# Last head's output split in place, first w_pm and w_out tiles leaving their last inputs to the end, sums of squares behind other products

## The chip, the cores and the metric

The kernel runs on one core of one Trainium2 chip. The metric is the time of one execution in microseconds on the device; a figure for a kernel is the median of several executions. The engines are named as the profile names them: PE (TensorE, matrix products; PEld is its weight load), DVE (VectorE), ACT (ScalarE), POOL (GpSimd) and SP (SyncE, which here only issues transfers). Each engine works through its own queue of instructions in order, and semaphores make it wait for others.

## The reference, cut to what matters

One layer of a diffusion backbone over 512 latent tokens of width 1024, with 256 context tokens, all in float32:

```python
h = rmsnorm(x, norm1_g) * (1 + sc1) + sh1
hm = head_norm(h_f + h_b, m_norm_g) * o          # mLSTM, 4 heads of width 256, forward and backward
hh = hyena(hv, (hx1, hx2), spec, hy_skip)        # long convolutions
y = gm * (hm @ w_pm) + gh * (hh @ w_ph)          # gated merge
x = x + g1 * (y @ w_out)
h2 = rmsnorm(x, norm2_g) * (1 + sc2) + sh2
x = x + g2 * ((silu(h2 @ w1) * (h2 @ w3)) @ w2)  # FFN, width 2816
return rmsnorm(x, final_g)
```

`g1`, `sh2`, `sc2` and `g2` are columns of `silu(c) @ w_ada + b_ada`. The change is about the way from the last head's `hm` through `w_pm` and `w_out` to `h2` and the first products of the FFN.

## The kernel before, in words

**Layout and products.** Features lie on the 128 partitions, tokens along the free axis; a tile is 128 features by 512 tokens, so a matrix of width 1024 is eight tiles (`KT` = 8). Each float32 operand is split into a high and a low part of a shorter type (`split`, lines 210 to 212: ACT copies the high part, DVE subtracts it for the low one), and each product is made of three PE instructions (`mm3`, lines 214 to 217, hence the lines 215 to 217 in the profile). An output tile is eight inputs times three products of 512 columns, accumulated in one PSUM bank (`gemm`, line 555); its list `ks` says which inputs, and the last product of each `gemm` is noted in `tails`. A block under `behind()` (line 560) puts the instructions that it issues behind the last noted product on PE's queue. Weights come by `wsplit` (line 221): SP loads a raw tile `wr` (four buffers), ACT and DVE split it into `wh` and `wl` (four buffers each).

**Order.** The program is traced as straight code, and a planner then orders the queue of each engine, by the order of tracing as priority and by estimated durations of instructions and transfers; it may pull later work forward into time that it believes free, but keeps the order that `behind()` asks for. Weight loads run at a higher priority. On the chip the queues run in the planned order, whether or not the estimate holds.

**The heads.** For each of four heads, `load_head` loads keys, queries and values (SP, line 894, through the same four `wr` buffers), `decay` builds decay tables, `weigh` multiplies them with the scores (DVE, line 924), `halves` splits the result, `values` makes the outputs of the two directions, and `head_norm` normalises them over a head's width on DVE and POOL (lines 955 to 959). `head_out` (line 961) then transposes the four token tiles on PE (line 965), scales them on ACT (line 968), multiplies them with the output gate that SP has loaded (DVE, line 971) and stores the two feature tiles of the head to DRAM as `hmd` (POOL, line 972). For head h it is called in the course of head h + 1; for the last head by `late()` behind the sixth of the eight `w_ph` tiles. These tiles (`ph_tiles`, line 1272) are spread over the heads as fill for PE. Tiles 0 to 5 of `hmd` are read back and split during the last head (line 1337).

**w_pm.** After the heads, tiles 6 and 7 of `hmd` (the last head's) are read back and split (`reload`, line 1368). Then come eight tiles of `w_pm`, each a whole `gemm`, and a merge: two loads, DVE lines 1379 and 1380, a split into `y`.

**w_out.** Five tiles of `w_out` as whole products, then the last three tiles (`LAST` = 3) in halves of 256 tokens: for each half three products, then the sum of squares over all features by products with ones (`half_rms`, lines 1403 and 1404), a power on POOL (line 373), its spread over the partitions by PE (line 375), and the eight tiles of `h2` for this half (DVE 1438, ACT 1439, DVE 1440). `out_tile` (lines 1390 to 1394) adds the residual and squares. Then the first three FFN tiles, `w1` 0, `w3` 0 and `w1` 1, are made by halves too (lines 1446 to 1450).

**Rows of the modulation matrix.** `background()` takes one step of `ada_later` (line 339): SP loads a 512 KB piece of `w_ada` into a `wr` buffer (line 344), and DVE multiplies the piece loaded before with a row and sums it (line 354). `ada_row` prepares that row. Such steps are called once ahead of the heads, after each `w_ph` tile, after each `w_pm` and `w_out` tile, and three times behind `w_out`; 24 pieces are needed by the end of `w_out`.

## Time and profile before

| | us |
|---|---|
| three runs | 1242.1, 1242.74, 1244.75 |
| median | 1242.74 |
| the profiled execution | 1246.66 |
| its span, first to last instruction | 1244.9 |
| PE busy | 1198.9 (96%) |
| DVE busy | 835.5 (67%) |
| ACT busy | 529.4 (43%) |
| mean granted clock of PE | 0.983 |

The span of the profiled execution starts at 0. The heads run from some 580 us to 755, `w_pm` to 815, `w_out` to 870, the FFN to the end. An engine's busy time says how much work it has; the idle time before an instruction, with what ended it, says what it waited for. The granted clock is 1.00 at full speed (2.4 GHz) and 0.50 at the lower level (1.2 GHz).

### The profile page before, as it was taken

The page shows a single profiled execution, that of the slowest core. Times are in us where ns is not written, and L with a number is a line of the kernel's source. Part 1 is how long each engine was busy: PE and PEld are TensorE (multiplying, and loading weights), DVE is VectorE, ACT ScalarE, POOL GpSimd, SP SyncE. Part 2 cuts the span into 40 slices and gives each one's busy share as a digit, 9 for nine tenths or more (in the row PEclk, how much of TensorE's full clock was granted, in tenths as well). Part 3 has the DMA queues.
Part 4 walks back from the last instruction along what each step waited for, and adds up shares of the span by engine and source line. Part 5 has one row for each costly group of instructions (what it writes and reads, how often), then busy time and mean ns, then how long its engine had stood idle before and what let it go on. Part 6 is the DMA issues. An engine that isn't in the chain of part 4 may idle for free.

```text
span 1244.9 us, 16797 instructions
## 1 busy us (share of the span) xinstructions
PE 1198.9 (96%) x6440; PEld 1020.4 (82%) x6440; DVE 835.5 (67%) x1336; ACT 529.4 (43%) x824; POOL 69.2 (6%) x135
## 2 busy tenths in 40 slices
PE   4999999999999999999999997999999999999997
PEld 2799988888888888887878885878988888888886
DVE  6967798979989899894597785765744433432332
ACT  3754556654445454446564532223422332222231
POOL 0011110100000000001010111000000000000000
PEclk9999999999999999999989997999999999999999
DMA  9644442554342443345435668764443233223312
GB/s 354 236 165 149 160 167 95 181 191 135 112 155 81 161 135 130 116 127 198 139 108 172 209 213 269 260 204 133 147 152 101 87 101 102 91 88 95 104 47 68
DMA packets 61585, 184.83 MB, mean 148 GB/s; under 512 B 8504, under 2 KB 12352, under 8 KB 59328
## 3 DMA queue, kind: packets, MB, share of 16 engines
q1 hardware_dynamic: 53840, 154.38, 38.1%
q0 software_dynamic: 7664, 29.37, 6.4%
q8 instruction: 51, 0.84, 0.3%
q14 instruction: 30, 0.25, 0.1%
HBM read 152.26 MB, written 31.46 MB: 148 GB/s over the span
## 4 chain that ended last, share of the span: by engine, by line
PE 86%; DMA 5%; DVE 4%; issue 2%; ACT 1%; POOL 1%; SPq 0%; DVEq 0%; POOLq 0%; ACTq 0%
PE bank L215 25%; PE bank L216 25%; PE bank L217 25%; DMA wr<-in_wada 3%; PE bank L641 2%; PE bank L642 2%; PE bank L643 2%; DMA s<-hmd 1%; PE bank L862 1%; DVE wl L212 1%; PE bank L445 1%; PE bank L598 1%; PE bank L446 1%; DMA wr<-in_wph 0%; DMA ul<-in_xT 0%
## 5 line engine op out<-in xcount | busy, mean ns | idle before, releaser
L215 PE MATMUL bank<-hTh,wh 128*128 128x512 f32 (+1 forms) x952 | 368.2, 389 | 3.8 <-ACT hTh L1065 2.0
L216 PE MATMUL bank<-hTl,wh 128*128 128x512 f32 (+1 forms) x952 | 367.9, 387 | 1.9 <-DVE hTl L1071 1.9
L217 PE MATMUL bank<-hTh,wl 128*128 128x512 f32 (+1 forms) x952 | 367.2, 386 | 0.0
L211 ACT ACTIVATE wh<-wr 128x1024 fp32r<-128x1024 f32 (+1 forms) x167 | 172.3, 1033 | 431.7 <-PE bank L216 223.1
L212 DVE TENSOR_TENSOR wl<-wr,wh 128x1024 fp32r<-128x1024 f32 (+1 forms) x167 | 198.1, 1188 | 183.0 <-ACT wh L211 181.2
L215 PEld LDWEIGHTS bank<-hTh,wh 128*128 128x128 f32 x952 | 179.7, 189 | 38.9 <-ACT hTh L1065 2.2
L216 PEld LDWEIGHTS bank<-hTl,wh 128*128 128x128 f32 x952 | 179.9, 189 | 36.6 <-DVE hTl L1071 2.4
L217 PEld LDWEIGHTS bank<-hTh,wl 128*128 128x128 f32 x952 | 179.8, 189 | 35.3 <-issue 0.2
L215 PE MATMUL bank<-big,wh 128*128 128x512 f32 (+1 forms) x266 | 96.1, 362 | 7.7 <-ACT big L211 7.7
L216 PE MATMUL bank<-big,wh 128*128 128x512 f32 (+1 forms) x266 | 96.6, 363 | 0.3 <-DVE big L212 0.3
L217 PE MATMUL bank<-big,wl 128*128 128x512 f32 (+1 forms) x266 | 96.0, 361 | 0.0
L215 PEld LDWEIGHTS bank<-big,wh 128*128 128x128 f32 x266 | 51.2, 193 | 15.8 <-ACT big L211 8.6
L216 PEld LDWEIGHTS bank<-big,wh 128*128 128x128 f32 x266 | 51.5, 194 | 8.0 <-DVE big L212 0.7
L217 PEld LDWEIGHTS bank<-big,wl 128*128 128x128 f32 x266 | 51.5, 194 | 7.3
L354 DVE SCALAR_TENSOR_TENSOR wr<-wr,crow 128x1024 f32<-128x1024 f32 x32 | 39.0, 1220 | 22.9 <-DMA wr<-in_wada 22.9
L211 ACT ACTIVATE hb<-hb 128x512 fp32r<-128x512 f32 (+1 forms) x49 | 36.7, 768 | 28.6 <-DVE hb L450 18.2
L1466 DVE TENSOR_TENSOR s<-s,bank 128x512 f32<-128x512 f32 x22 | 15.1, 686 | 46.8 <-PE bank L217 46.8
L212 DVE TENSOR_TENSOR hb<-hb,hb 128x512 fp32r<-128x512 f32 (+1 forms) x49 | 40.3, 858 | 2.0 <-ACT hb L211 1.8
L641 PE MATMUL bank<-wh,hTh 128*128 128x256 f32 (+1 forms) x128 | 36.4, 284 | 0.0
L643 PE MATMUL bank<-wh,hTl 128*128 128x256 f32 (+1 forms) x128 | 36.4, 284 | 0.0
L642 PE MATMUL bank<-wl,hTh 128*128 128x256 f32 (+1 forms) x128 | 36.4, 284 | 0.0
L373 POOL TENSOR_TENSOR rr<-rv,negh 128x2 f32<-128x2 f32 (+1 forms) x6 | 4.5, 756 | 526.4 <-DVE rv L371 526.4
(376 smaller groups left out, 2200.7 us busy)
## 6 DMA issues: line engine op xcount, KB each, us to landing
wr<-in_win SPq DMA_DIRECT2D x64, 512.0 KB, 3.7
wr<-in_w SPq DMA_DIRECT2D x60, 512.0 KB, 3.7
wr<-in_wada SPq DMA_DIRECT2D x32, 512.0 KB, 4.4
Kd<-K POOLq DMA_DIRECT2D x8, 1024.0 KB, 4.7
K<-Kd SPq DMA_DIRECT2D x8, 1024.0 KB, 5.8
wr<-in_wv SPq DMA_DIRECT2D x8, 512.0 KB
gmd<-s POOLq DMA_DIRECT2D x16, 256.0 KB, 2.7
wr<-in_wph SPq DMA_DIRECT2D x8, 512.0 KB, 3.7
```

The costliest lines, as they stand in the source:

```text
L211: act.activation(hi, x, AF.Copy)
L212: dve.tensor_sub(lo, x, hi.bitcast(F32))
L215: pe.matmul(o, wh, xh, start=first, stop=False)
L216: pe.matmul(o, wh, xl, start=False, stop=False)
L217: return pe.matmul(o, wl, xh, start=False, stop=last)
L354: dve.scalar_tensor_tensor(w, w, 1.0, crow[:], op0=ALU.mult, op1=ALU.mult, accum_out=s)
L445: pe.matmul(ps[:], lhs, w4h, start=True, stop=False)
L446: pe.matmul(ps[:], lhs, w4l, start=False, stop=True)
L641: pe.matmul(o, xh, wh, start=bool(k == 0), stop=False)
L642: pe.matmul(o, xh, wl, start=False, stop=False)
L643: m = pe.matmul(o, xl, wh, start=False, stop=bool(k == KT - 1))
L1466: dve.tensor_tensor(t[:], t[:], pb[:], op=ALU.mult)
```

## The change

- `head_out` gets `keep`: with it the two tiles are not stored but handed back.
- The last head's `head_out` is called behind the seventh `w_ph` tile instead of the sixth, with `keep`; its two tiles are split where they are, as inputs 6 and 7 of `w_pm`, before the eighth `w_ph` tile is traced. The reload of these two goes.
- `staged_gemms`: the first n output tiles run their first inputs only, all n; then each runs the remaining inputs, in order, and is finished. For `w_pm` n is 3, with inputs 6 and 7 left to the end; for `w_out` n is 2, with input 7 left.
- In the halves of the last three `w_out` tiles, the first tile of the second half is made before the first half's sum of squares, which is put behind it; the second half's sum is traced after the first FFN half product and put behind it.
- The calls of `background()`: `ada_row` is moved ahead of the first `weigh`; two steps each follow the first `weigh` and the next two fills, and one step follows each `beside`. Those after the `w_ph` tiles, after the first two `w_pm` tiles and behind `w_out` go. Their number stays 25 in all.

```diff
@@ -958,7 +958,8 @@
             gp.tensor_tensor(rs[:], rs[:], negh[:, :1], op=ALU.pow)
             dve.tensor_scalar(hs[:, t], hs[:, t], mv[:, 0:1], rs[:], op0=ALU.subtract, op1=ALU.mult)
 
-    def head_out(h, hs):
+    def head_out(h, hs, keep=False):
+        kept = []
         pt = [bank(), bank()]
         for t in range(4):
             for i in range(2):
@@ -969,7 +970,11 @@
             o = T(PM_, [128, SEQ], F32, "s2")
             dma(o[:], od[:, 2 * h + i])
             dve.scalar_tensor_tensor(hg[:], o[:], 1.0, hg[:], op0=ALU.add, op1=ALU.mult)
-            store(hmd[:, 2 * h + i], hg[:])
+            if keep:
+                kept.append(hg)
+            else:
+                store(hmd[:, 2 * h + i], hg[:])
+        return kept
 
 
     P1 = ExitStack()
@@ -1279,7 +1284,6 @@
             dma(g[:], gmd[:, 1, d])
             dve.scalar_tensor_tensor(g[:], g[:], 1.0, ps[:], op0=ALU.add, op1=ALU.mult)
             store(y2d[:, d], g[:])
-            background()
             yield
 
     fill(next(cf))
@@ -1298,23 +1302,31 @@
         L = heads.get(h) or load_head(h)
         return L, [decay(h, d) for d in range(2)]
 
+    def steps(n):
+        for _ in range(n):
+            background()
+
     L, Dm = start(0)
     fill(next(cf))
+    ada_row()
     weigh(0, L[0], L[1], Dm)
+    steps(2)
     fill(next(cf))
-    ada_row()
+    steps(2)
     W = [halves(Dm[d]) for d in range(2)]
     fill(next(cf))
+    steps(2)
     while fills:
         fill(1)
+        steps(2)
     ph = ph_tiles()
-    background()
     PHN = ((1, 0), (1, 1), (1, 1), (0, 0))
     done = []
 
     def beside(h, i):
         for _ in range(PHN[h][i]):
             next(ph)
+        steps(1)
 
     def late(_=None):
         if done:
@@ -1347,9 +1359,9 @@
         if nxt:
             L, W = nxt[0], Wn
     next(ph)
-    late()
-    for _ in ph:
-        pass
+    next(ph)
+    with behind():
+        ends = head_out(*done.pop(), True)
     PMS.close()
 
 
@@ -1365,13 +1377,36 @@
     def half(t, hf):
         return t[:, 256 * hf : 256 * hf + 256]
 
-    rest = reload(hmd, big, big, range(6, KT))
-    hm = hm[0] + rest[0], hm[1] + rest[1]
+    for t in ends:
+        hi, lo = big(), big()
+        split(hi[:], lo[:], t[:])
+        hm[0].append(hi)
+        hm[1].append(lo)
+    for _ in ph:
+        pass
+
+    def staged_gemms(key, xs, n, last, finish, total, each=1):
+
+        opened = []
+        for d in range(total):
+            wh, wl = wsplit(I[key][d], [128, KT, 128])
+            ps = bank(psG)
+            if d < n:
+                gemm(ps, wh, wl, *xs, SEQ, range(last))
+                opened.append((ps, wh, wl))
+                if d < n - 1:
+                    continue
+                for j, (ps, wh, wl) in enumerate(opened):
+                    with behind():
+                        gemm(ps, wh, wl, *xs, SEQ, range(last, KT))
+                    finish(j, ps)
+            else:
+                gemm(ps, wh, wl, *xs, SEQ)
+                finish(d, ps)
+
     y = ([], [])
-    for d in range(KT):
-        wh, wl = wsplit(I["wpm"][d], [128, KT, 128])
-        ps = bank(psG)
-        gemm(ps, wh, wl, hm[0], hm[1], SEQ)
+
+    def merge(d, ps):
         g = scr()
         dma(g[:], gmd[:, 0, d])
         t = scr()
@@ -1381,7 +1416,10 @@
         y[0].append(big())
         y[1].append(big())
         split(y[0][-1][:], y[1][-1][:], g[:])
-        background()
+        if d > 1:
+            background()
+
+    staged_gemms("wpm", hm, 3, 6, merge, KT)
     dve.tensor_scalar_mul(g1h[:], modT[:, 2, :, 0], 0.5)
 
 
@@ -1414,30 +1452,38 @@
     for d in range(KT):
         xr.append(scr())
         dma(xr[-1][:], I["xT"][:, d])
-        if d < KT - LAST:
-            wh, wl = wsplit(I["wout"][d], [128, KT, 128])
-            ps = bank(psG)
-            gemm(ps, wh, wl, y[0], y[1], SEQ)
-            out_tile(ps, SEQ, d, g1h, 0, xr[d], x1[d], acc1)
-            background()
-    for _ in range(LAST):
+
+    def project(d, ps):
+        out_tile(ps, SEQ, d, g1h, 0, xr[d], x1[d], acc1)
         background()
+
+    staged_gemms("wout", y, 2, KT - 1, project, KT - LAST)
     dve.scalar_tensor_tensor(am2[:], modT[:, 4, :, 0], 1.0, n2g, op0=ALU.add, op1=ALU.mult)
     ws = [wsplit(I["wout"][d], [128, KT, 128]) for d in range(KT - LAST, KT)]
     h2 = ([slots("hTh")() for _ in range(KT)], [slots("hTl")() for _ in range(KT)])
-    for hf in range(2):
-        for d in range(KT - LAST, KT):
-            wh, wl = ws[d - KT + LAST]
-            ps = bank(psG)
-            gemm(ps, wh, wl, [half(t, hf) for t in y[0]], [half(t, hf) for t in y[1]], 256)
-            sq = out_tile(ps, 256, d, g1h, 256 * hf, xr[d], x1[d], acc1)
-        rb = half_rms(acc1, sq, hf)
+
+    def last_tile(hf, d):
+        wh, wl = ws[d - KT + LAST]
+        ps = bank(psG)
+        gemm(ps, wh, wl, [half(t, hf) for t in y[0]], [half(t, hf) for t in y[1]], 256)
+        return out_tile(ps, 256, d, g1h, 256 * hf, xr[d], x1[d], acc1)
+
+    def norm2(hf, sq):
+        with behind():
+            rb = half_rms(acc1, sq, hf)
         for k in range(KT):
             t = scr()
             sh = modT[:, 3, k, 0:1]
             dve.scalar_tensor_tensor(t[:, :256], half(x1[k], hf), am2[:, k : k + 1], rb[:, :256], op0=ALU.mult, op1=ALU.mult)
             act.activation(half(h2[0][k], hf), t[:, :256], AF.Identity, bias=sh)
             dve.scalar_tensor_tensor(half(h2[1][k], hf), t[:, :256], sh, half(h2[0][k], hf).bitcast(F32), op0=ALU.add, op1=ALU.subtract)
+
+    for d in range(KT - LAST, KT):
+        sq = last_tile(0, d)
+    sq1 = last_tile(1, KT - LAST)
+    norm2(0, sq)
+    for d in range(KT - LAST + 1, KT):
+        sq1 = last_tile(1, d)
     ff = ([], [])
     later = ada_later(3 * KT, 4 * KT)
     lead = {}
@@ -1446,6 +1492,8 @@
     for hf in range(2):
         for (n, f), (wh, wl) in zip(jobs, wlead):
             if hf == 0:
+                if len(lead) == 1:
+                    norm2(1, sq1)
                 lead[n, f] = bank(psG)
             gemm(half(lead[n, f], hf), wh, wl, [half(t, hf) for t in h2[0]], [half(t, hf) for t in h2[1]], 256)
```

## Rows read from the trace of the kernel before

**Rows 1.** The page's parts 1 and 2: busy time of each engine and its share of the span; PE's granted clock in 40 slices of the span, in tenths.

```profile
PE 1198.9 (96%) x6440; PEld 1020.4 (82%) x6440; DVE 835.5 (67%) x1336; ACT 529.4 (43%) x824; POOL 69.2 (6%) x135
...
PEclk9999999999999999999989997999999999999999
```

**Rows 2.** The waits of PE over the whole span: line that waited, engine and tile waited for, us in total, times, longest.

```profile
PE bank L215 <- ACT big L211: 7.7, 2, 5.5
...
PE bank L965 <- DVE hs L959: 4.4, 3, 3.0
PE bank L1403 <- DVE s L1394: 2.2, 1, 2.2
```

**Rows 3.** Busy time in chosen stretches: start:end, length, then busy us and count of PE, PEld, DVE, ACT and POOL; granted clock, DMA share, GB/s.

```profile
744.58:767.41 22.83, 18.91 (x76) 14.86 (x74) 15.44 (x30) 6.75 (x9) 6.07 (x8) 0.85 0.77 253
767.41:773.07 5.66, 0.17 (x2) 0.01 (x1) 0.60 (x3) 0.63 (x1) 0.00 (x0) 0.94 0.80 258
773.07:779.20 6.13, 6.13 (x15) 4.79 (x16) 3.25 (x5) 1.69 (x2) 0.00 (x0) 0.50 0.88 313
819.99:823.89 3.90, 1.37 (x5) 0.68 (x5) 3.57 (x6) 0.63 (x1) 0.00 (x0) 0.96 0.82 251
823.89:826.90 3.01, 3.01 (x7) 2.44 (x8) 1.94 (x4) 1.69 (x2) 0.00 (x0) 0.50 0.97 351
```

**Rows 4.** PE in order of time around the last head's transposes (L965) and where w_pm meets the reloaded tiles. Columns: start, duration, engine, line, operation, out<-in, shape, count; in brackets the idle time before it and what ended it.

```profile
744.58 0.38 PE L965 MATMUL bank<-mats,hs 128*128 128x128 f32 x2
...
750.25 0.69 PE L965 MATMUL bank<-mats,hs 128*128 128x128 f32 x2 [3.04 <-DVE hs L959]
...
756.75 0.38 PE L965 MATMUL bank<-mats,hs 128*128 128x128 f32 x2
...
757.66 0.39 PE L215 MATMUL bank<-hTh,wh 128*128 128x512 f32 x1
...
773.07 0.80 PE L215 MATMUL bank<-big,wh 128*128 128x512 f32 x1 [5.49 <-ACT big L211]
```

**Rows 5.** DVE in the same stretch: a row of the modulation matrix (L354), head_norm's last step (L959), head_out's products (L971).

```profile
753.23 1.23 DVE L354 SCALAR_TENSOR_TENSOR wr<-wr,crow 128x1024 f32<-128x1024 f32 x1 [0.53 <-DMA wr<-in_wada]
...
754.91 0.41 DVE L959 TENSOR_SCALAR hs<-hs,mv,rs 128x256 f32<-128x256 f32 x1 [0.45 <-POOL rs L958]
...
761.01 1.29 DVE L971 SCALAR_TENSOR_TENSOR s<-s,s 128x512 f32<-128x512 f32 x2
```

**Rows 6.** POOL and then SP: the store of the last head's two tiles, and the load of the same two.

```profile
762.00 1.15 POOL L972 DMA_DIRECT2D hmd<-s  x2 [7.12 <-DVE s L971]
...
767.38 0.96 SPq L1260 DMA_DIRECT2D s<-hmd  x2
```

**Rows 7.** PE where eight transposes of an earlier head stood together, and a product behind them.

```profile
658.80 1.04 PE L965 MATMUL bank<-mats,hs 128*128 128x128 f32 x8
...
659.92 0.40 PE L216 MATMUL bank<-hTl,wh 128*128 128x512 f32 x1
```

**Rows 8.** PE and then DVE where w_pm ends and w_out begins.

```profile
815.01 0.39 PE L217 MATMUL bank<-big,wl 128*128 128x512 f32 x1
...
819.77 0.39 PE L217 MATMUL bank<-big,wl 128*128 128x512 f32 x1
822.38 0.73 PE L215 MATMUL bank<-big,wh 128*128 128x512 f32 x2 [2.22 <-ACT big L211]
...
818.70 1.22 DVE L354 SCALAR_TENSOR_TENSOR wr<-wr,crow 128x1024 f32<-128x1024 f32 x1
...
823.15 0.69 DVE L212 TENSOR_TENSOR big<-s,big 128x512 fp32r<-128x512 f32 x1
```

**Rows 9.** PE and then DVE around the two halves' sums of squares and the first FFN products.

```profile
856.58 0.28 PE L217 MATMUL bank<-big,wl 128*128 128x256 f32 x1
...
870.26 0.28 PE L215 MATMUL bank<-hTh,wh 128*128 128x256 f32 x1
...
876.00 0.50 PE L1403 MATMUL bank<-mats,s 128*128 128x1 f32 x4
...
889.12 0.40 PE L215 MATMUL bank<-hTh,wh 128*128 128x512 f32 x1
...
855.65 1.23 DVE L354 SCALAR_TENSOR_TENSOR wr<-wr,crow 128x1024 f32<-128x1024 f32 x1 [3.73 <-DMA wr<-in_wada]
...
862.40 0.87 DVE L1438 SCALAR_TENSOR_TENSOR s<-K,am,bank 128x256 f32<-128x256 f32 x2 [2.12 <-PE bank L375]
...
874.49 0.47 DVE L1440 SCALAR_TENSOR_TENSOR hTl<-s,modT,hTh 128x256 fp32r<-128x256 f32 x1
...
878.85 1.26 DVE L1438 SCALAR_TENSOR_TENSOR s<-K,am,bank 128x256 f32<-128x256 f32 x3 [1.58 <-PE bank L375]
```

**Rows 10.** DVE in the first head's stage, the same stretch's busy time (columns as in rows 3), and the idle time of DVE before line 354 over the whole span (us, times).

```profile
594.47 2.58 DVE L924 SCALAR_TENSOR_TENSOR dx<-bank,dx 128x512 f32<-128x512 f32 x4 [12.01 <-PE bank L217]
...
588.00:592.00 4.00, 4.00 (x18) 2.91 (x18) 0.00 (x0) 4.00 (x13) 0.00 (x0) 1.00 0.00 0
...
  DMA wr<-in_wada: 22.9, 14
```

**Rows 11.** Busy time in a stretch of the heads' stage (columns as in rows 3), and PE at a wait in the same stage.

```profile
644.65:656.20 11.55, 10.98 (x38) 8.54 (x39) 8.59 (x24) 7.93 (x21) 3.06 (x4) 0.56 0.45 149
...
719.01 0.47 PE L215 MATMUL bank<-hTh,wh 128*128 128x512 f32 x1 [1.77 <-DVE den L944]
```

## The prediction, made before the changed kernel was run

> **What bounds the kernel now.** I read four views. First the page: PE is busy for 96% of the span, so nothing but PE's own idle or slow time can be won [rows 1]. The clock line shows where to look: two dips, one in the middle (the heads) and none in the long FFN part; full speed is 2.4 GHz, half of it 1.2. Second, the waits of PE: the long ones after the start are the reloaded tiles (big, 7.7 us with 5.5 in one piece), the last head's transposes (hs, 4.4), and the sum of squares (s, 2.2) [rows 2]. Third, busy time by stretch, to see what each wait costs besides itself: behind the 5.66 us gap at 767.41 the granted clock is 0.50 for 6.13 us, so half of that, 3.07, is lost too; behind the gap at 819.99 it is 0.50 for 3.01 us, 1.5 lost [rows 3]. Fourth, the engines in order of time at these places. The full rate is (819.77 - 815.01) / 21 = 0.227 us per product of 512 columns [rows 8]; a tile of 24 takes 5.44.
>
> **The change, part by part.**
>
> *The last head in place (A).* Now the two tiles of head 3 are multiplied on DVE at 761.01, stored by POOL at 762.00, loaded by SP at 767.38, and the first PE product that uses them starts at 773.07 after 5.49 us of idle [rows 4 to 6]. The change drops two stores and two loads (four issues, 256 KB each), keeps the same two splits, and lets the first three w_pm tiles run inputs 0 to 5 first: 3 x 18 x 0.227 = 12.3 us of products that need nothing of head 3, behind the eighth w_ph tile (5.44). The in-place chain is L971 until 762.3, then two splits, of which DVE's half takes 0.69 each (823.15, rows 8) behind ACT's: some 2.1 us in all, ready near 764.4. The inputs would be wanted near 757.66 + 5.44 + 12.3 = 775.4 on the present clock. Cover 11 us, so both the gap and the slow stretch go: 5.66 + 3.07 = **8.7**. If DVE put a row and its DMA wait (1.23 + 3.73, rows 9) ahead, 6 us of cover would be left. Nothing is late next: the finishing parts are 3 x 6 products, and the weights of tile 4 need the buffer pair that tile 0 frees 1.4 us into them, with 2 x 1.4 + 5.44 = 8.2 us to go.
>
> *The transposes one tile later (D).* They stand behind the sixth w_ph tile now; tile 7 is broken up by them. From 744.58 to 757.66 tile 7 and eight transposes take 13.08 us; at full rate they would take 5.44 + 0.9 [rows 4, 7], so 6.7 are lost, to waits for hs and a clock of 0.85 over the stretch [rows 3]. Behind tile 7 they come due at 744.58 + 5.44 = 750.0. But hs of the last token tile is written at 754.91 + 0.41 = 755.3, held by a row on DVE that itself waited for its DMA (753.23) [rows 5]. Everything behind the transposes on PE waits for that: 5.3 us in one piece, and as behind 767.41 a slow stretch of 3.07. Then tile 8 has lost 8.4 instead of 6.7 (a loss of 1.7). If hs came by 750.0 the gain would be the whole 6.7. A gap as short as 1.77 us [rows 11] was followed by full speed; with hs 2 us sooner the gain would be 3.4. Nearest to the rows is hs unchanged, but five matrix rows leave this stage for the first head's, so I take **0** between -1.7 and 6.7.
> By the Trainium skill (TensorE: Matmul & The Clock Gate, section "Part 4: PE-mode transpose") transposes do not count as work for the clock gate, so eight of them in one block would leave the clock down and cost another 3.07, 1232.7 in all. The trace does not bear this out: behind eight together at 658.80 the next product takes 0.40 us, the full-rate duration [rows 7, 8]. So the sum has none of it.
>
> *The first two w_out tiles (B).* The last w_pm product starts at 815.01; its merged tile is split at 823.15 + 0.6 = 823.8, late because rows of the matrix (818.70 among them) stand between its steps on DVE [rows 8]. PE idles 3.90 - 1.37 = 2.5 us and then loses 1.5 [rows 3]. Two tiles without their last input give 2 x 21 x 0.227 = 9.5 us, until 824.8: one us more than needed. **4.0**, at least 0 if a row with its DMA wait (5 us) stands in the way, not more than 4.0.
>
> *Sums of squares (C).* Between 856.7 and 870.26 PE did three half tiles and the small products in 13.5 us; the FFN's six lead products, twice that work, took 889.12 - 870.26 = 18.86, so 9.4 would have done: 4.0 lost [rows 9]. The change puts the sums behind a half tile of 2.9 us. But DVE sets what follows. The sums would start at 859.6 instead of 859.0, so the first half's normalising at 863.0 instead of 862.40, and it takes 874.49 + 0.47 - 862.40 = 12.6 us, because weight splits and the last tiles share DVE: 875.6. The second half's sums must now follow the whole first lead product, whose last inputs are that 875.6: 0.4 us of products, then 2.85 as from 876.00 to 878.85: the second half's normalising starts at 878.8, as now. PE then still has 72 products, 8.6 us, and 0.5 until the first input: 888.0, against 889.12. So of 4.0 only 1.1 is gained; the other 2.9 become a new gap in the lead products. As behind 819.99, that may slow PE and take 1.5 back: -0.4. I take **0.4**, with ends 4.0 and -1.5 (a further row on DVE, 1.22).
>
> *Rows of the matrix moved forward (E).* Five rows and a load more go to the first head's stage: DVE waits 12.01 us before 594.47 and the DMA share is 0.00 at 588 [rows 10]; 5 x 1.23 = 6.1 us fit. Their loads stand on SP ahead of the second head's, and share four buffers with them. Later stages have fewer rows. The nearest wait that they could relieve is 1.77 [rows 11]. I take **0**, between 1.8 gained and the rivals below. The three background steps dropped behind w_out, and those of the w_ph tiles, are the same rows at other places.
>
> **Sum.** 8.7 + 0 + 4.0 + 0.4 + 0 = 13.1. The profiled execution took 1246.66 (span 1244.9), 3.9 above the median; it would be 1233.6. From the median, 1242.74 - 13.1 = **1229.6**.
>
> **The rivals.**
> *hs comes in time.* For it: five rows leave DVE's queue. Against: the waits for the reload of the third head stay. 1229.6 - 6.7 = 1222.9.
> *A new stall in the heads.* There PE has almost no idle, but DVE is full, and in one stretch from 644.65 an idle time of 0.57 was followed by slow products, a clock of 0.56 over 11.55 us, 5.1 lost [rows 11]. The planner orders all queues anew, and one more such stall and D at its lower end give 1229.6 + 5.7 + 1.7 = 1237.0; two give 1242.7, no change.
> *Slower: rows ahead of the first head's weighting.* If the five rows land on DVE behind 594.47 and ahead of the halves that PE waits for, each costs 1.23 and its wait for the load, 22.9 / 14 = 1.6 [rows 10]: 14.3, and a slow stretch of 3.07: 1229.6 + 17.4 = 1247.0. From 13.1 on it decides. Against: the 12 us hole and the idle DMA come first.
> The Trainium skill (PSUM — Partial Sum Buffer, section "Engine vs sequencer instructions") says that the queues of ScalarE and VectorE are strict FIFO, so that such a row holds all behind it. The trace agrees: a row that waited 3.73 us at 855.65 held the tiles behind it and so the sums [rows 2, 9]. With a queue that could be overtaken this rival would fall away.
> *It does not do what it says.* That the split in place hides nothing would need head 3 more than 11 us later than now; I leave it no chance of its own.
>
> **How the numbers follow.** A measurement of this kernel tells 0.2% (2.5 us) from no change. Forecast 0.55, own range 1224 to 1234 (C at 4.0 and some of D below; B gone above). hs in time 0.15. One stall 0.16, two 0.07 (the case of no change). Slower 0.07. Faster: 0.55 + 0.15 + 0.16 = 0.86; same 0.07; slower 0.07. The range 1220 to 1241 leaves out the slower case, the two stalls and a little of hs in time.
>
> **What would show it.** A: no wait of PE for big near the w_pm start, no L972 store for the last head. B: no wait of PE at w_out's first tile. D: eight L965 behind tile 7 with a wait for L959 of 2 to 5 us. C: no wait at L1403 of the first half, but one of hTh or hTl in the lead products. E: five L354 before 600. The prediction is wrong if the heads' stage (580 to 740) lengthens by more than 3 us, or if a wait for big remains.

## The result, and the profile after

The changed kernel took 1237.11 us (median of four, 1236.85 to 1238.27), the kernel before beside it 1243.74 (four, 1242.1 to 1245.43): a ratio of 0.9948 [0.9931, 0.9966], 6.6 us faster. Forecast were 1229.6 and a gain of 13.1, with a range of 1220 to 1241: the time lies within the range, the gain is half of the forecast. In a second comparison (e9 below) the same kernel took 1232.19 against 1246.4, 0.9900 [0.9873, 0.9927]. The title names three parts of the change; a further one, the moved rows of the modulation matrix, turned out to matter as much.

The page of the kernel after, parts 1 and 2 (compare [rows 1]), and the waits of PE that changed or are new (columns as in [rows 2]):

```profile
PE 1196.6 (97%) x6440; PEld 1019.4 (82%) x6440; DVE 835.0 (68%) x1336; ACT 529.4 (43%) x824; POOL 68.2 (6%) x133
...
PEclk9899999999999999999998998999999999999998
```

```profile
PE bank L966 <- DVE hs L959: 5.7, 3, 3.3
PE bank L375 <- POOL rr L373: 3.0, 3, 1.1
PE bank L215 <- DVE dx L924: 2.5, 1, 2.5
...
PE bank L215 <- ACT hTh L1478: 0.5, 1, 0.5
```

Line 966 is the old 965 (transposes), 1478 the old 1439. The waits for big, 7.7 us before, are gone, and so are the one for the sums of squares and the 1.77 us for `den` (line 944, a head's denominators) at 719.01 [rows 11]. New are a wait for dx (the weighting of a later head) and the small ones behind the sums. To see where the time went, cut both spans at the same PE instructions: the wait near 645 us, the first w_ph product behind it, the first w_pm product, the first half tile of w_out, the second input of the first whole FFN product (not the first: in the new order the planner puts one product of it ahead). Columns as in [rows 3]; first the kernel after, then the kernel before.

```profile
645.85:660.84 14.99, 14.42 (x68) 12.14 (x68) 9.27 (x30) 8.68 (x25) 3.05 (x4) 0.66 0.57 182
660.84:767.79 106.95, 98.77 (x548) 84.45 (x547) 80.93 (x187) 46.88 (x90) 14.74 (x30) 0.95 0.58 189
767.79:838.51 70.72, 70.72 (x314) 58.56 (x313) 44.32 (x61) 20.76 (x26) 0.54 (x1) 1.00 0.72 242
838.51:880.51 42.00, 40.34 (x317) 39.48 (x315) 29.69 (x61) 16.84 (x31) 2.44 (x2) 0.96 0.29 88
880.51:1236.50 355.99, 346.84 (x1600) 289.91 (x1598) 136.96 (x168) 96.79 (x123) 1.39 (x2) 0.99 0.32 99
```

```profile
644.65:659.59 14.94, 14.37 (x67) 11.93 (x68) 9.27 (x30) 8.70 (x25) 3.06 (x4) 0.66 0.55 181
659.59:763.11 103.52, 97.40 (x548) 83.53 (x547) 83.24 (x192) 45.03 (x88) 15.98 (x31) 0.97 0.60 202
763.11:846.99 83.88, 75.86 (x314) 61.46 (x313) 50.01 (x70) 22.23 (x27) 1.12 (x3) 0.94 0.73 237
846.99:889.82 42.83, 40.18 (x316) 39.51 (x315) 29.68 (x61) 17.52 (x31) 1.42 (x2) 0.96 0.35 107
889.82:1244.90 355.08, 346.33 (x1600) 289.50 (x1598) 136.65 (x167) 96.58 (x123) 1.39 (x2) 0.99 0.32 99
```

Read the second column (length), the third (PE busy) and the clock. w_pm and w_out lose 83.88 - 70.72 = 13.16 us and have no idle time left. The heads give 3.43 of it back (106.95 for 103.52), in idle time (8.18 for 6.12) and in clock (0.95 for 0.97). The 2.06 of idle time are, but for 0.04, 2.49 for dx and 1.30 more at the third head's transposes (1.73 for 0.43), less the 1.77 for `den`. 1.2 more lie ahead of 645, but executions of the same lines differ as much there (644.65 in this profile of the kernel before, 646.00 in that of e14). The sums gain 0.83, the FFN loses 0.91, with no edit in it.

How the new wait in the heads comes about, on four queues of the kernel after (SP, ACT, DVE, PE; the first number is the start, the second the duration), with SP of the kernel before ahead of them:

```profile
688.48 0.33 SPq L236 DMA_DIRECT2D wr<-in_wph  x1
690.01 0.33 SPq L344 DMA_DIRECT2D wr<-in_wada  x1
694.74 0.33 SPq L236 DMA_DIRECT2D wr<-in_wph  x1
...
695.95 0.33 SPq L344 DMA_DIRECT2D wr<-in_wada  x1
...
701.80 0.33 SPq L236 DMA_DIRECT2D wr<-in_wph  x1
```

```profile
689.82 0.33 SPq L236 DMA_DIRECT2D wr<-in_wph  x1
691.35 5.06 SPq L344 DMA_DIRECT2D wr<-in_wada  x2
...
697.23 0.33 SPq L344 DMA_DIRECT2D wr<-in_wada  x1
...
701.22 0.33 SPq L236 DMA_DIRECT2D wr<-in_wph  x1
...
703.91 0.33 SPq L236 DMA_DIRECT2D wr<-in_wph  x1
```

```profile
705.34 1.06 ACT L211 ACTIVATE wh<-wr 128x1024 fp32r<-128x1024 f32 x1 [4.48 <-DMA wr<-in_wph]
710.46 1.06 ACT L211 ACTIVATE wh<-wr 128x1024 fp32r<-128x1024 f32 x1 [4.06 <-DMA wr<-in_wph]
```

```profile
699.96 1.22 DVE L354 SCALAR_TENSOR_TENSOR wr<-wr,crow 128x1024 f32<-128x1024 f32 x1 [2.03 <-DMA wr<-in_wada]
...
702.65 1.23 DVE L354 SCALAR_TENSOR_TENSOR wr<-wr,crow 128x1024 f32<-128x1024 f32 x1 [0.85 <-DMA wr<-in_wada]
...
711.55 1.23 DVE L212 TENSOR_TENSOR wl<-wr,wh 128x1024 fp32r<-128x1024 f32 x1 [2.65 <-ACT wh L211]
712.69 0.69 DVE L924 SCALAR_TENSOR_TENSOR dx<-bank,dx 128x512 f32<-128x512 f32 x1
```

```profile
713.53 0.76 PE L215 MATMUL bank<-uh,K 128*128 128x512 f32 x1 [2.49 <-DVE dx L924]
714.09 0.63 PE L216 MATMUL bank<-ul,K 128*128 128x512 f32 x1
```

Before, the loads of w_ph (line 236) and of w_ada (line 344) take turns on SP. After, three pieces of w_ada stand between two weights of w_ph. The next two w_ph loads are issued at 701.22 and 703.91, each within 0.05 us of the end of a row's product on DVE (699.96 and 702.65), which gives a `wr` buffer back, and each of these products had itself waited for its own load. ACT then waits 4.48 and 4.06 us for the two weights, DVE's low part (711.55) waits for ACT, and the weighting of the next head, which has nothing to do with w_ph, stands behind that low part on DVE. PE waits 2.49 us for it, and its next products take 0.63 us where 0.39 is the full rate. By the Trainium skill (PSUM — Partial Sum Buffer, section "Engine vs sequencer instructions") VectorE's queue is strictly first in, first out. The trace agrees: line 924 starts as soon as the waiting line 212 lets it, at 712.69.

### The profile page after: what moved, and what is told of

Read it like the earlier page. It is cut to its first block, busy times and chain, and to the rows that moved or that the text cites. A ratio compares the mean times of both kernels' runs of the same rounds, so it can differ in the third digit from the quotient of the medians.

```text
span 1236.5 us, 16783 instructions
## 1 busy us (share of the span) xinstructions
PE 1196.6 (97%) x6440; PEld 1019.4 (82%) x6440; DVE 835.0 (68%) x1336; ACT 529.4 (43%) x824; POOL 68.2 (6%) x133
## 3 DMA queue, kind: packets, MB, share of 16 engines
q1 hardware_dynamic: 53552, 153.86, 38.3%
## 4 chain that ended last, share of the span: by engine, by line
PE 90%; DMA 5%; DVE 3%; ACT 1%; issue 1%; POOL 1%; SPq 0%; DVEq 0%; POOLq 0%; ACTq 0%
PE bank L215 27%; PE bank L216 26%; PE bank L217 26%; PE bank L641 2%; PE bank L643 2%; PE bank L642 2%; DMA wr<-in_wph 1%; PE bank L862 1%; PE bank L445 1%; PE bank L598 1%; DMA mats<-in_mats 1%; PE bank L446 1%; DMA hb<-in_dftf 1%; DMA hmd<-s 1%; DMA K<-in_wada 0%
## 5 line engine op out<-in xcount | busy, mean ns | idle before, releaser
L354 DVE SCALAR_TENSOR_TENSOR wr<-wr,crow 128x1024 f32<-128x1024 f32 x32 | 39.0, 1222 | 26.3 <-DMA wr<-in_wada 26.2
```

The source lines that it names most:

```text
L354: dve.scalar_tensor_tensor(w, w, 1.0, crow[:], op0=ALU.mult, op1=ALU.mult, accum_out=s)
```

## The experiments

Every kernel was timed beside the kernel before on its chip. All are gathered here; the ratio is to that kernel before. The last four columns are from one profiled execution each, cut at the instructions named above: the stretch from the wait near 645, the heads behind it (in brackets PE's idle time there: the window's length less PE's busy time), w_pm and w_out, and the sums up to the second input of the first whole FFN product. (The expectations below end the last stretch three products of 512 columns earlier where the order of the sums is the old one; their 42.1, 39.4 and 38.3 are 42.8, 40.1 and 39.0 here.) A profiled execution can be far from its kernel's median: e2's (1236.27) is 4.9 us below it.

| | what it has of the change | median us | ratio | 645 | heads | w_pm, w_out | sums |
|---|---|---|---|---|---|---|---|
| before | nothing | 1243.74 | 1 | 14.94 | 103.52 (6.1) | 83.88 | 42.83 |
| after | all | 1237.11 | 0.9948 [0.9931, 0.9966] | 14.99 | 106.95 (8.2) | 70.72 | 42.00 |
| e9 | all, second comparison | 1232.19 | 0.9900 [0.9873, 0.9927] | 10.77 | 103.70 (7.1) | 70.72 | 40.50 |
| e1 | all but the rows | 1228.40 | 0.9870 [0.9848, 0.9893] | 14.97 | 102.20 (5.3) | 70.72 | 42.01 |
| e2 | rows alone | 1241.13 | 0.9959 [0.9943, 0.9975] | 10.77 | 106.93 (9.0) | 73.36 | 42.50 |
| e3 | split in place, w_pm | 1234.88 | 0.9909 [0.9886, 0.9933] | 14.97 | 100.38 (3.8) | 77.50 | 40.08 |
| e4 | w_out alone | 1236.12 | 0.9920 [0.9894, 0.9945] | 14.95 | 101.34 (4.9) | 78.41 | 39.02 |
| e5 | all but rows and sums | 1224.29 | 0.9836 [0.9808, 0.9865] | 10.77 | 102.05 (5.6) | 70.72 | 39.64 |
| e6 | e5, transposes behind tile 8 | 1226.50 | 0.9853 [0.9826, 0.9880] | 14.94 | 97.40 (2.5) | 72.33 | 39.91 |
| e7 | all, rows beside the values undone | 1228.87 | 0.9862 [0.9831, 0.9893] | 14.86 | 102.00 (5.5) | 70.72 | 42.01 |
| e8 | all, six early rows undone | 1233.67 | 0.9903 [0.9876, 0.9929] | 14.94 | 100.51 (5.5) | 70.72 | 40.50 |
| e10 | all, 8 rows not multiplied | 1232.88 | 0.9905 [0.9881, 0.9930] | 10.59 | 103.29 (6.5) | 70.72 | 40.50 |
| e11 | all, 8 rows not loaded | 1230.72 | 0.9880 [0.9856, 0.9904] | 14.84 | 101.30 (3.6) | 70.72 | 40.51 |
| e12 | e6 with the six early rows | 1224.76 | 0.9831 [0.9806, 0.9856] | 14.94 | 96.70 (2.2) | 71.18 | 39.74 |
| e13 | all but the sums | 1228.85 | 0.9878 [0.9853, 0.9903] | 10.79 | 105.49 (7.5) | 70.72 | 39.40 |
| e14 | sums alone | 1246.14 | 0.9996 [0.9974, 1.0018] | 14.95 | 103.30 (5.6) | 84.13 | 40.84 |

**The parts alone.** e1 puts the calls of `background()` and `ada_row()` back to where the kernel before has them; e2 makes that move alone:

```diff
             store(y2d[:, d], g[:])
+            background()
             yield
...
-    steps(2)
...
+    background()
     PHN = ((1, 0), (1, 1), (1, 1), (0, 0))
...
             next(ph)
-        steps(1)
...
-        if d > 1:
-            background()
+        background()
...
     staged_gemms("wout", y, 2, KT - 1, project, KT - LAST)
+    for _ in range(LAST):
+        background()
```

> The changed kernel with the rows of the modulation matrix called where the kernel before calls them; all else as changed. Theory R (the rows moved into the heads cost what the trace shows between 645 and 740 us, 4.1 us beyond the 0.7 that the two executions already differ by at their 582 us): 1237.1 - 4.1 = 1233.0, and PE's first product of w_pm's reach (743.93 in the changed kernel) comes near 739.8. Theory P (the loss in the heads comes from the new order of everything else, the rows being innocent): unchanged, 1236 to 1238. Theory S (the rows had to leave w_pm and w_out for the in-place split and the staged tiles to gain in full, since a row with its DMA wait on DVE holds the finishing steps): the heads are back but w_pm and w_out together lose up to 5 of the 13.1 won, 1236 to 1238 too, with waits of PE for big at w_pm or w_out telling it from P.

> The kernel before with nothing changed but the calls for the rows of the modulation matrix. Theory R: slower by about 4.1, 1247.8, the loss between 645 and 740. Theory P: as before within 1, 1243 to 1245. Theory S: slower in the heads by 4 and faster behind them (fewer rows between the merge steps on DVE), so about 1244 to 1246.

e3 and e4 are the kernel before with one part each, e3 with the first of these edits, e4 with the second:

```diff
-    late()
+    next(ph)
+    with behind():
+        ends = head_out(*done.pop(), True)
...
-    rest = reload(hmd, big, big, range(6, KT))
...
+    staged_gemms("wpm", hm, 3, 6, merge, KT)
```

```diff
+    staged_gemms("wout", y, 2, KT - 1, project, KT - LAST)
```

> The kernel before with the last head's split in place and the three staged w_pm tiles alone; rows, w_out and sums of squares as before. Theories R and P on its share: the part is worth the 8.6 seen in w_pm, 1243.7 - 8.6 = 1235.1, minus or plus what the transposes one tile later bring (0.1 in the changed kernel). Theory S: rows at the first two w_pm tiles stand before the splits on DVE and take up to 5 back, 1240.

> The kernel before with the two staged w_out tiles alone, rows between the tiles as there. Forecast term 4.0, seen in the changed kernel 4.55: 1243.7 - 4.5 = 1239.2, no wait of PE for big near 820. If a row with its DMA wait stands in the way (Theory S), 0 to 2: 1242 to 1243.7.

e1 came to 1228.4, 16.4 below the kernel before on its chip. Theory R gave it 4.1 less than the changed kernel; it is 8.7 lower by the first comparison's number, and by the second's ratio 0.3% (4 us), with intervals that meet. P falls: the loss in the heads goes with the rows (idle 8.2 and 7.1 with all of the change, 5.3 here). S falls as well, w_pm and w_out are 70.72 with the rows back among them, and PE is never idle there (but what S said of the rows alone is the shape of e2).

e2 was a surprise: the rows alone make the kernel 3.65 us faster, not 4.1 slower. They do cost the heads their 3.4 (106.93), but behind the heads they gain 83.88 - 73.36 = 10.5 (6.3 of it idle time, the rest clock): the wait at w_pm's start falls from 5.49 [rows 4] to 1.27, and the one at w_out's start is gone. PE of e2 where w_pm meets the reloaded tiles, and then PE of e3 where w_out meets the last merged tile:

```profile
768.59 0.50 PE L215 MATMUL bank<-big,wh 128*128 128x512 f32 x1 [1.27 <-ACT big L211]
```

```profile
813.34 0.49 PE L215 MATMUL bank<-big,wh 128*128 128x512 f32 x1 [4.04 <-ACT big L211]
814.42 0.75 PE L216 MATMUL bank<-big,wh 128*128 128x512 f32 x1 [0.58 <-DVE big L212]
```

In e3 the wait at w_pm is gone as forecast, but w_out's first tile now waits 4.04 + 0.58 where it waited 2.22 [rows 8]: w_pm ends 10.9 us earlier, the last merged tile comes only 9.5 earlier, behind a row that waits 2.49 us for its load (DVE, 810.07). e4 gained twice what was expected, 8.7 us by the medians: to its 5.5 here come 3.8 in the sums, where the stall on the late row is gone. So over this stretch three parts each gain alone (rows 10.5, split in place 83.88 - 77.50 = 6.4, w_out 83.88 - 78.41 = 5.5), together 22.4, of which only 13.16 are there to be had; split in place and w_out without the rows (e1) already have all 13.16.

**The sums and the transposes.** e5 is e1 with the old loop over the halves. e6 is e5 with this edit, and without the later loop over `ph`:

```diff
-    next(ph)
-    next(ph)
+    for _ in ph:
+        pass
     with behind():
         ends = head_out(*done.pop(), True)
```

> The kernel of e1 with the sums of squares also as before: only the split in place and the staged w_pm and w_out tiles are left of the change. From PE's first half product of w_out to the first whole FFN product the changed kernel took 42.0 us, e1 42.0, the kernel before 42.1, but e3 and e4, whose sums are as before and which have no row waiting for its DMA there, 39.4 and 38.3. Theory N (the new order of the sums costs what it saves, and a kernel without the late row is better off with the old order): 1228.4 - 3 = 1225.4, and 38 to 39.5 in that stretch. Rival (the stretch is short in e3 and e4 for another reason, such as the stall just ahead of it): 42 again, 1228.4.

> e5 with the last head's transposes behind the eighth w_ph tile instead of the seventh. In e1 and e3 PE still waits 2.3 to 2.8 us at these transposes and is slow behind them, and from the first of them to the first w_pm product goes 11.4 and 10.5 us where 5.44 + 0.9 would do: 4 to 5 lost. Theory D (the staged w_pm tiles cover 12.3 us and the chain from the transposes to the two splits takes some 7, so a tile may be spent): e5 - 4.5, no wait at the transposes, none for big. Rival: the chain is longer than the cover, a wait for big of 2 or more in w_pm, e5 or slower.

e5: 1224.29 and 39.64 in the last stretch, as theory N said, against e1's 1228.40 and 42.01; the intervals of the two meet, and 1.5 of the 2.4 us in the stretch are clock (at full clock the new order takes 40.50). e6: half right. The heads are 4.7 shorter, as theory D said (97.40, idle 2.5), but w_pm and w_out are 1.6 longer, with waits of 0.39 for a low weight part and 0.49 for big, and the median is not below e5's; the intervals overlap.

**Which rows.** e7 has the six early ones only (the other eight go behind the w_ph tiles), e8 the eight beside the values only (the other five go behind w_pm's first two tiles and w_out, as before):

```diff
             store(y2d[:, d], g[:])
+            background()
             yield
...
             next(ph)
-        steps(1)
```

```diff
     weigh(0, L[0], L[1], Dm)
-    steps(2)
     fill(next(cf))
-    steps(2)
...
+    background()
     PHN = ((1, 0), (1, 1), (1, 1), (0, 0))
```

> The changed kernel with the eight steps beside the heads' values moved back behind the w_ph tiles; the six early ones in the first head's stage stay. Theory B (the steps beside the values put w_ada loads on SP ahead of the w_ph loads and cost the heads): PE from the wait near 645 to w_pm's first product as in e1, 5 less than in the changed kernel, 1232. Theory F (the six early ones shift the loads of all later rows): as the changed kernel, 1237.

> The changed kernel with the six early steps undone (one ahead of the heads, two more after the first two w_pm tiles, three behind w_out, as before); the eight steps beside the values stay. Theory B: the heads as slow as in the changed kernel, 1237. Theory F: 1232. If both e7 and e8 are fast, only the two together overfill the four wr buffers.

By the medians theory B holds: e7 stands with e1 (0.9862 and 0.9870), e8 with the changed kernel (0.9903 and 0.9900), though the intervals of e7 and e8 meet and both times are some 3 us below those expected. The profiles are not as clear. e7 has e1's idle time in the heads (5.5), but e8's profiled execution has it too, and a full clock there; at 1229.62 it was the fastest of e8's six, the others took 1232.66 to 1235.94. So the six early rows cost nothing that can be seen, as was forecast for the hole on DVE; what the other eight cost without them, the profile of e8 leaves open.

**The loads or the products.** e9 is the changed kernel again; in e10 and e11 the eight steps beside the values run with half of their work each (`MODE` is set during these steps; e10's edit first). Without its load a step multiplies the row vector with itself, and e11 leaves out all the pieces of w_ada that are loaded between 600 and 720 us, as many as the kernel before loads there (eight):

```diff
+            if MODE[0]:
+                dve.tensor_scalar_mul(s, w[:, 0:1], 1.0)
+            else:
+                dve.scalar_tensor_tensor(w, w, 1.0, crow[:], op0=ALU.mult, op1=ALU.mult, accum_out=s)
```

```diff
-                nxt = wada(j + 1)
+                nxt = None if MODE[0] else wada(j + 1)
...
+            v = crow[:] if w is None else w
+            dve.scalar_tensor_tensor(v, v, 0.0 if w is None else 1.0, crow[:], op0=ALU.mult, op1=ALU.mult, accum_out=s)
```

> The changed kernel itself again, beside e10 to e12 on one chip. Every theory: 1237 within 2, and again PE waits for dx L924 near 713 and for hs near 737; if the loss in the heads were a matter of the one execution profiled first, these waits would not come back.

> The changed kernel with the products of the eight rows beside the values left out (their loads stay, the piece is read by a product of one column, so that buffers are taken and given back in the same order; eight entries of the modulation vectors are wrong). Theory L (the loads do it: they stand ahead of the w_ph loads on SP and take wr buffers): most of the loss stays, 1235 to 1237, with PE's wait for dx L924. Theory V (the 1.23 us on DVE does it, 8 of them in stages where DVE is full): heads as in e1 and e7, about 1229 to 1231.

> The changed kernel with the loads of eight rows beside the values left out, the products staying (they multiply the row vector with itself instead, so the modulation vectors are wrong). Theory L: heads as in e1 and e7, 1229 to 1231, no wait for dx L924. Theory V: as the changed kernel, 1235 to 1237.

ACT's waits for w_ph and PE's waits for hs (the transposes) and for the weighting, of e9, e10 and e11 in this order (in e10 lines 966 and 924 have become 971 and 929; in e11 966 is 969):

```profile
ACT wh L211 <- DMA wr<-in_wph: 15.9, 6, 5.5
...
PE bank L966 <- DVE hs L959: 5.6, 3, 3.3
...
PE bank L215 <- DVE dx L924: 1.5, 1, 1.5
```

```profile
ACT wh L211 <- DMA wr<-in_wph: 16.0, 6, 4.1
...
PE bank L971 <- DVE hs L964: 5.3, 3, 3.3
```

```profile
ACT wh L211 <- DMA wr<-in_wph: 4.9, 2, 4.5
...
PE bank L969 <- DVE hs L962: 2.7, 2, 1.9
```

e9 itself is 5 us below the 1237 that was expected; the two waits came back. Theory L holds in part. Without the products ACT still waits 16.0 us for the w_ph weights, and PE's idle time in the heads falls by 0.7 only (7.1 to 6.5), but its wait for dx falls to 0.47. Without the loads ACT's waits fall to 4.9, PE waits for dx nowhere, and its idle time there is 3.6. In the medians the difference is 2.2 us (1232.88 and 1230.72 on one chip), within the intervals.

But e11 shows what the loads cost wherever they stand, not what moving them costs: ACT waits 12.1 us for w_ph in the kernel before and 12.5 in e1, with the same eight loads. What the move brought is in SP's own waits, of the kernel after between 680 and 716 us (the first number is the sum, then how often and the longest):

```profile
SPq L236 <- DVE wr L354: 3.9, 2, 3.2
```

A w_ph load waits for a row's product to give its buffer back. Between 640 and 722 us this wait stands in the six kernels with steps beside the values that load (3.9 to 5.4 us in the changed kernel, e9, e2, e8 and e13, 1.6 in e10), and in none of the other ten. PE's wait for dx stands in the same six and in no other: 0.9 to 2.5 us, 0.5 in e10.

**Six early rows with the transposes last.** e12 has the edits of e6 and e7 together.

> e6 with six rows moved into the first head's stage, as in e7, so that fewer of them stand between the steps of w_pm on DVE: from w_pm's first product to the first half tile of w_out e6 took 72.3 where e5 and e7 took 70.7, with short waits for DVE (wl, big) in w_pm. If the rows there cause them: 70.7 again, 1226.5 - 1.6 = 1224.9, and below e5 by up to 3 in executions whose clock stays up near 645. If not: as e6.

As expected: 1224.76, the stretch of w_pm and w_out 71.18 (expected were 70.7) and the heads the shortest of all (96.70). With e5 it is the fastest kernel here, 1.7% below the kernel before and below the changed kernel in both comparisons; e5 and e12 can't be told apart by their medians. e12's executions went down to 1220.58, e5's to 1223.08.

**The sums, in the changed kernel and alone.** e13 takes these lines out of the changed kernel, whose old loop over the halves comes back; e14 puts them into the kernel before:

```diff
-    sq1 = last_tile(1, KT - LAST)
-    norm2(0, sq)
...
-                if len(lead) == 1:
-                    norm2(1, sq1)
```

> The changed kernel with the sums of squares as before. Theory N (the new order costs in the changed kernel too: 42.0 and 40.5 us in its two profiles from the first half tile of w_out to the first whole FFN product, against 38.3 to 39.4 with the old order wherever no row's DMA wait stands there): 38 to 39.5 in that stretch, and 2 to 3 below the changed kernel's 1232 to 1237. Rival (with the rows where the change puts them, a row stands in the way of the old order as in the kernel before): 41 to 42, no difference.

> The kernel before with the new order of the sums alone. Forecast's term: 0.4 gained, between 1.5 lost and 4.0 gained; the stretch 42.1 before. Theory N: with the late row the old order lost 2.2 to a wait, the new one hides it and loses about as much at L375 and in the lead products, so 40 to 42 and no difference beyond 1 us, 1243 to 1246.

e13 fits theory N. e14 is no different from the kernel before; in its profile the stretch is 2.0 us shorter than before's (40.84 for 42.83), 1.1 of it busy time, since the clock stayed up, but w_out's first tile waits 4.24 there. The stretch in three pieces (first half tile of w_out, first sum, first lead product, end as above) at full clock, of e9 with the new order and of e13 with the old one:

```profile
831.11:842.62 11.51, 11.51 (x97) 11.51 (x96) 7.37 (x13) 2.81 (x5) 0.00 (x0) 1.00 0.42 137
842.62:851.12 8.50, 7.36 (x63) 7.15 (x62) 6.13 (x13) 3.73 (x6) 1.74 (x1) 1.00 0.21 64
851.12:871.61 20.49, 19.97 (x161) 19.32 (x160) 16.20 (x36) 10.30 (x20) 0.70 (x1) 1.00 0.24 78
```

```profile
832.02:841.05 9.03, 8.79 (x73) 8.58 (x71) 6.94 (x13) 2.39 (x4) 0.00 (x0) 1.00 0.40 117
841.05:851.86 10.81, 10.33 (x85) 10.13 (x86) 7.22 (x16) 4.65 (x8) 0.72 (x1) 1.00 0.31 99
851.86:871.42 19.56, 19.56 (x161) 19.30 (x160) 15.82 (x35) 10.27 (x19) 0.70 (x1) 1.00 0.27 84
```

The new order has no wait for the sums, but one of 1.14 behind them (8.50 - 7.36), for the spread through POOL, and 0.52 among the lead products (20.49 - 19.97). The old order, without a late row ahead of it, waits 0.24 for the sums (9.03 - 8.79) and 0.48 behind them (10.81 - 10.33), nothing later. That makes 40.50 against 39.40, 1.1 us, and 2.6 where the clock falls at the new order's wait (42.00, the changed kernel's first profile).

## Why the prediction was right or wrong

**A, the last head in place, 8.7: right.** w_pm took 52.1 us (763.11 to 815.24) and takes 43.5; 8.6. Nothing waits for big. Alone (e3) the same 8.6 is worth 6.4, since w_out gives 2.2 back; the sum was right to price A and B together.

**B, w_out, 4.0: right.** 31.75 became 27.20, 4.55. The forecast saw one microsecond of spare cover; it was enough, even with the rows back (e1).

**D, the transposes, 0: right in the changed kernel.** From the sixth w_ph tile to w_pm 23.99 became 23.86. hs of the last token tile is as late as forecast, PE waits 0.62 and 3.34, and the clock falls behind it. Its upper end lay in another place: the transposes behind tile 8 gain 4.7 in the heads (e6), 5.3 with the six early rows (e5 to e12), though no median shows it: the ratios of e5, e6 and e12 are 0.9836, 0.9853 and 0.9831. (In the forecast's reading of the eight transposes at 658.80 it is the second product behind them that takes 0.40 us; the first takes 0.50.)

**C, the sums, 0.4 between -1.5 and 4.0: right against the kernel before, of the wrong sign in the changed one.** The traces show 0.83 gained, and alone (e14) it is 0.9996, nothing that can be measured. But the term priced the old order behind a row that waits 3.73 us for its DMA [rows 9]. With the w_out tiles staged that stall is gone or short (idle time in the whole stretch 2.65 before, 0.5 in e4, 0.7 in e13), and then the old order takes 39.0 to 39.9 and the new one 40.5 to 42.0. Against the changed kernel without it (e13) the edit costs 1.1 to 2.6 us in the profiles; the medians point the same way (0.9878, against 0.9900 and 0.9948), with intervals that meet the nearer one's.

**E, the rows moved forward, 0: the step that failed.** The words were "The nearest wait that they could relieve is 1.77" and "I take **0**, between 1.8 gained and the rivals below". Both halves were off. The rows relieve 10.5 us of waits behind the heads (e2); B itself had put w_out's wait down to rows between the merge's steps. But A and B already remove these waits, so that this gain is nothing here (70.72 in e1, with the rows back). And they cost more in the heads than the 1.77, which they did relieve. The forecast counted five rows of 1.23 us against a hole on DVE, which fits (six stand before 600 us, one in the kernel before, and e7 shows no cost), and it named the shared buffers for these five alone. For the others, "the same rows at other places", it had no price, and their place on SP is what costs: eight pieces are loaded between 600 and 720 us before and after, but three of them now stand in a row, and w_ph loads wait 3.9 to 5.4 us for buffers that rows hold. PE's idle time in the heads is 7.1 to 8.2 us with them (after, e9, e13), 4.9 to 6.1 in the kernel before, e4 and e14, 5.3 to 5.6 in e1, e5 and e7. e8 stands against this with 5.5 in its one profile. Undone, the kernel takes 1228.4 (e1), 0.9870 of the kernel before: by the ratios E costs 4 us (e9) to 10 us (the first comparison), so its size is known only roughly.

**The forecast of the whole.** It gave the rival "a new stall in the heads" 1237.0 and a chance of 0.16, and that is the time that the first comparison found. The time is luck in part: the rival was 5.7 for a stall and 1.7 for D, and what came was 3.4 in the heads and nothing from D. The stall was of another kind than the rival's idle time of 0.57: PE idles 2.49 us at the end of a wait for a buffer, and is slow behind it. What was named as the sign against the forecast also came: from the first product of line 835 to the sixth w_ph tile 157.7 us became 161.8, over the 3 that were allowed. Summed over the profiled executions: 8.6 (A) + 4.55 (B) + 0.83 (C) + 0.13 (D) - 4.8 (up to the sixth w_ph tile, 0.7 of it at line 835 already, so perhaps not the rows' doing) - 0.9 (the FFN) = 8.4, and 1246.66 - 1238.27 = 8.39. The other 1.8 to the medians' 6.6 is the two profiled executions' distance from their medians, 2.9 and 1.2.

**What stays open.** Why the two comparisons differ by half a per cent. The kernel's ten executions run from 1229.15 to 1238.27 with their mean clock from 0.995 to 0.984, and the four of the first comparison all have 0.984 to 0.986. Whether that is chance or the chip was not settled; the record does not name the chip of the first. With e9's ratio the forecast of 13.1 is within the interval (1246.4 x 0.0073 to 0.0127 is 9 to 16 us); but then by luck: E and C cost time in that execution too (idle 7.1 in the heads, 40.50 for the sums), and what makes up for them is clock that the forecast did not count on.

## What to carry to other kernels

Ask of a moved step where its load will stand, and not only where its arithmetic fits: here six rows of 1.23 us fitted a hole on DVE, while the loads of others, no more of them than before but three in a row, held up another engine's weights through a shared ring of buffers. Several edits that each remove the same wait don't add up; price them in the order in which they would be made, and ask of each whether the others have left anything for it. An edit that breaks even while something else is late can cost 1 to 3 us once that is mended (the sums, in the profiles), so each part is tried last by taking it out of the finished whole.

## What the runs showed of the hardware

**The same wait, with and without a slow stretch.** Near 645 us every profile of these kernels has the same two gaps on PE (0.49 to 0.77, and 0.56 or 0.57) among the same products. In eleven of the sixteen profiles the granted clock then falls and the stretch takes 14.8 to 15.0 us at 0.65 or 0.66, in five it stays at 1.00 and the stretch takes 10.6 to 10.8. e6 and e5, the same lines up to here:

```profile
644.55:659.49 14.94, 14.37 (x68) 11.85 (x68) 9.27 (x30) 8.68 (x25) 3.05 (x4) 0.66 0.56 174
```

```profile
644.91:655.68 10.77, 10.20 (x67) 8.50 (x67) 9.08 (x30) 8.47 (x25) 3.06 (x4) 1.00 0.46 151
```

So a difference of 4 us between two executions is within what one place does by itself, and a comparison of profiles has to name the clock of each stretch. Idle time repeats better: 0.57 here in all sixteen but one (0.56), and within some 1.2 us over the heads of the same lines (6.1, 4.9 and 5.6 in the kernel before, e4 and e14).

**Transposes and the clock, once more.** In e6 eight transposes stand in one block with a wait of 1.92 us in it. PE of e6, and the stretch behind:

```profile
753.96 0.82 PE L966 MATMUL bank<-mats,hs 128*128 128x128 f32 x6
756.70 0.44 PE L966 MATMUL bank<-mats,hs 128*128 128x128 f32 x2 [1.92 <-DVE hs L959]
756.89 0.47 PE L215 MATMUL bank<-K,wh 128*128 128x512 f32 x1
757.21 0.39 PE L216 MATMUL bank<-K,wh 128*128 128x512 f32 x1
```

```profile
757.00:762.00 5.00, 5.00 (x25) 4.12 (x24) 2.97 (x4) 1.27 (x2) 0.54 (x1) 1.00 0.80 247
```

The second product behind them runs at the full rate, and the clock stays at 1.00. The Trainium skill (TensorE: Matmul & The Clock Gate, section "Part 4: PE-mode transpose") says that transposes do not count as busy in the way that other products do. Eight of them, with a wait among them, show no sign of it here, nor do the fourteen of line 835 in the kernel before (581.44, 1.69 us; the clock is 1.00 from there to 587).
